# Moving both parts of split activations through TensorE as one 512-column operand in a two-block transformer kernel

## The chip, the cores and the metric

The kernel runs on one core of one Trainium2 chip. The metric is the device time in microseconds from one launch; lower is better. Every number below is from one profiled execution of the kernel before, or from the three timed runs beside it.

## The reference, cut to what matters

Two transformer blocks run on 256 tokens of width 1024, in float32. All the matrix products that the change touches are projections of the 256 tokens through a weight matrix:

```python
def first_block(x, ...):
    xn = rms_norm(x, norm1_w[l])
    z = xn @ w_in[l]                       # q, k, v, xr, gr, g_a, g_b
    attn = nsa_attention(q, ...)
    rnn = rg_lru_branch(xr, gr, ...)
    merged = jax.nn.sigmoid(g_a) * (attn @ w_up_attn[l]) + jax.nn.sigmoid(g_b) * (rnn @ w_up_rnn[l])
    x = x + merged @ w_out[l]
    hn = rms_norm(x, norm2_w[l])
    x = x + jnp.square(jax.nn.relu(hn @ mlp_w1[l])) @ mlp_w2[l]
    return rms_norm(x, final_norm_w)

def second_block(x, c, ...):
    for layer in range(2):
        sh1, sc1, g1, sh2, sc2, g2 = ...   # from c
        h = rmsnorm(x, norm_mix[layer]) * (1.0 + sc1) + sh1
        y = even_mixer(h, ...) if layer % 2 == 0 else odd_mixer(h, ...)   # both end in "@ w_out"
        x = x + g1 * y
        h = rmsnorm(x, norm_ffn[layer]) * (1.0 + sc2) + sh2
        x = x + g2 * peer_ffn(h, peer_w_q[layer], ...)                    # q = ht @ w_q, then 16384 experts
    return rmsnorm(x, norm_final)
```

## The kernel before, in words

**Layout.** Activations stand transposed: 128 features in the partitions, 8 chunks of features, 256 tokens in the columns. `T` is 256 and `KC` is 8.

**Split precision.** Every float32 operand is a sum of two fp32r tiles, an upper part and the rest. `Split` (L164 and after) loads a weight block of 128 x 8 x 128 with one DMA and makes two halves of it. For each half ScalarE casts the upper part (`wh`, L183) and VectorE subtracts it (`wl`, L184). The list `HI` (L39) says for each phase which share of the casts goes to VectorE instead (L181); only phase 5, the MLP, has a share, 0.4. The pools `ws` (5, and one more in most stages) hold the halves, so the two engines can be some halves ahead of TensorE.

**A product.** `mm3` (L195 to L199) takes three matmuls for one chunk: `wh` with the upper activations `hh` (L197), `wh` with the rest `hl` (L198), `wl` with `hh` (L199). Each has 256 columns, loads its own weights, and adds into the same 256 columns of a PSUM bank. I call three such matmuls a trio. `proj` runs the 8 trios of one block of 128 outputs into a bank of the pool `pm`, which has two banks; `proj_pairs` does the same for the mixers' output projections with 4 trios to a bank, because the 8 chunks come in two halves. After a block `filler()` advances side work by a rate: routing, gates, the ada products on GpSimd (L472), the recurrence.

**Who empties a bank.** In the gates (L788, L793) a VectorE copy; in `w_out` (L811) and `mlp2` (L875) one VectorE addition onto `x`; in the mixers' outputs (L1050, L1210) one VectorE multiply-add onto `x`; in the MLP's first product a ScalarE Relu (L865), then a VectorE square (L867) and a split into `hdh`, `hdl` (L240, L241); in the PEER query product a ScalarE copy (`evac`, L86).

**After `x`.** `norm_lead` makes from each chunk of `x` an upper part `rh` (ScalarE, L328) and a rest `rl` (VectorE, L329), takes squares (ScalarE, L253) and sums them (VectorE, L257). With `rh` and `rl` it runs four projections before the norm's factor is known (the leads), then makes `hh` and `hl`.

**Order.** Each engine runs its own list in a fixed order that is made when the kernel is built, from the order in the code and from what depends on what; so a later step is often placed among earlier ones of other chains.

**Memory.** `act_pair` gives two tiles, `hh` and `hl`. In the PEER part the same two places hold `av` (activations of experts read back from memory) in turn, and then `nat`.

Of the kernel before, what the change touches and what calls it, by code (L numbers as in the profile page):

```python
# [20 lines left out]
T = 256  # L21
# [17 lines left out]
HI = 0.0, 0.0, 0.0, 0.0, 0.0, 0.4, 0.0, 0.0  # L39
# [26 lines left out]
def build(tc, a, dbg=None):  # L66
    nc = tc.nc
    es = ExitStack()
    with es:
# [142 lines left out]

        def proj_nat(src, ah, al, n, o=None, pool_=None, head=None):

            o = o or [bank(pool_ or pm) for _ in range(2)]
            nb = src.shape[0]
            for g in range(nb):
                w = head if g == 0 and head is not None else Split(src[g], [128, 2, n])
                for k in range(2):
                    for tt in range(2):  # L220
                        ts = slice(tt * 128, tt * 128 + 128)
                        kk = 2 * g + k
                        mm3(o[tt][:, :n], ah[:, kk, ts], al[:, kk, ts], *w[k], kk == 0, kk == 2 * nb - 1)
                filler()
            return o

        def proj_pairs(src, ah, al, k0):

            for f in range(2 * src.shape[0]):
                if f % 2 == 0:  # L230
                    w = Split(src[f // 2], [128, 2, 4, 128])
                o = bank(pm)
                for k in range(4):
                    mm3(o[:, :T], *(x[:, k] for x in w[f % 2]), ah[:, k0 + k], al[:, k0 + k], k == 0, k == 3)
                if f % 2 == 1:
                    filler()
                yield f, o
# [146 lines left out]
        def act_pair():  # L384
            oh = act.tile([128, KC, T], F32R, tag="hh", name="hh")
            ol = act.tile([128, KC, T], F32R, tag="hl", name="hl")
            return oh, ol
# [129 lines left out]
        xh, xl = act_pair()  # L517

        with tc.tile_pool(name="fb", bufs=1) as fb, ExitStack() as fs:
# [266 lines left out]
            for c in range(KC):  # L786
                o = proj(win(16 + c), xh, xl)
                nc.vector.tensor_copy(gr[:, c], o[:, :T])  # L788
            ga = fb.tile([128, KC, T], F32, name="ga")
            gb = fb.tile([128, KC, T], F32, tag="gb", name="gb")  # L790
            for c in range(2 * KC):
                o = proj(win(24 + c), xh, xl)
                nc.vector.tensor_copy((ga if c < KC else gb)[:, c % KC], o[:, :T])  # L793
# [3 lines left out]
            mh, ml = act_pair()  # L797
# [11 lines left out]
            for f in range(KC):  # L809
                o = proj(a["w_out"][f], mh, ml)  # L810
                nc.vector.tensor_tensor(out=cur["x"][:, f], in0=o[:, :T], in1=cur["x"][:, f], op=ALU.add)  # L811
# [42 lines left out]
        hh, hl = act_pair()  # L854
        with tc.tile_pool(name="mlp", bufs=1) as mp:
# [4 lines left out]
            hdh = mp.tile([128, 32, T], F32R, name="hdh")  # L860
            hdl = mp.tile([128, 32, T], F32R, name="hdl")
            for c in range(32):
                o = m4[:, c] if c < 4 else proj(a["mlp1"][c] if c > 4 else w4, hh, hl)
                r = t1.tile([128, T], F32, tag="t", name="r")
                nc.scalar.activation(r, o[:, :T], AF.Relu)  # L865
                q = t1.tile([128, T], F32, tag="t", name="q")
                nc.vector.tensor_tensor(out=q, in0=r, in1=r, op=ALU.mult)  # L867
                split_act(hdh[:, c], hdl[:, c], q)
            with tc.tile_pool(name="toe", bufs=1) as toe:
                side = beside(toeplitz(toe), 0.5)  # L870
                for f in range(KC):
                    o = bank(pm)
                    for kg in range(4):
                        proj(a["mlp2"][4 * f + kg], hdh, hdl, k0=8 * kg, o=o, first=kg == 0, last=kg == 3)
                    nc.vector.tensor_tensor(out=cur["x"][:, f], in0=o[:, :T], in1=cur["x"][:, f], op=ALU.add)  # L875
# [20 lines left out]
        def even_mixer(lp, m, sh, gcol):  # L896
            with tc.tile_pool(name="ev", bufs=1) as ev, ExitStack() as es2:
# [4 lines left out]
                hh, hl = act_pair()  # L902
# [144 lines left out]
                def mixed(products, n):  # L1047

                    for f, o in islice(products, n):
                        nc.vector.scalar_tensor_tensor(out=cur["x"][:, f], in0=o[:, :T], scalar=gcol[:, f:f + 1],  # L1050
                                                       in1=cur["x"][:, f], op0=ALU.mult, op1=ALU.add)
# [12 lines left out]
                for h in range(4):  # L1064
                    if h < 3:
                        qk_diff(h + 1)
                    if h == 2:

                        mh, ml = act_pair()
                        for tt in range(2):  # L1070
                            to_mix(ew, aos[tt].rearrange("p h d -> p (h d)"), mh, ml, 0, tt)
                        halves = [proj_pairs(a["ew_out"][half], mh, ml, 4 * half) for half in range(2)]
# [51 lines left out]
        def odd_mixer(lp, m, sh, gcol):  # L1124
            with tc.tile_pool(name="od", bufs=1) as od, ExitStack() as es2:
# [3 lines left out]
                hh, hl = act_pair()  # L1129
# [30 lines left out]
                mh, ml = od.tile([128, KC, T], F32R, name="mh"), od.tile([128, KC, T], F32R, name="ml")  # L1160
# [47 lines left out]
                for half in range(2):  # L1208
                    for f, o in proj_pairs(a["ow_out"][half], mh, ml, 4 * half):
                        nc.vector.scalar_tensor_tensor(out=cur["x"][:, f], in0=o[:, :T], scalar=gcol[:, f:f + 1],  # L1210
                                                       in1=cur["x"][:, f], op0=ALU.mult, op1=ALU.add)
# [148 lines left out]
        def peer(lps, lp, l, m, sh, gcol):  # L1360
# [9 lines left out]
            hh, hl = act_pair()  # L1370
# [26 lines left out]
            for c in range(4, 16):  # L1397
                o = proj(a["peer_w_q"][l, c] if c > 4 else w4, hh, hl)
                evac(qT[:, c], o[:, :T])
# [40 lines left out]
            for n, i2 in enumerate((124, 125, 126, 127)):  # L1440
                weigh([(i2, abs_[i2 // 2][:, i2 % 2])], n == 0, False)
            for n, b in enumerate([15] + list(range(15))):
                m = 4 if b == 15 else 8
                av = act.tile([128, 8, T], F32, tag=("hh", "hl")[n % 2], name="av")
# [9 lines left out]
            nat = act.tile([128, 2, 2, 512], F32, tag="hh", name="nat")  # L1454
# [160 lines left out]
```

## Time and profile before

| | us |
|---|---|
| median of 3 timed runs | 2439.26 (2437.25 to 2440.48) |
| the profiled execution | 2435.75 |
| its span, first to last instruction | 2434.0 |
| TensorE busy in the span | 2361.3 (97%) |
| VectorE busy in the span | 2130.1 (88%) |
| ScalarE busy in the span | 1706.7 (70%) |
| GpSimd busy in the span | 726.0 (30%) |

The profile shows one execution. Between its span and its own time lie 1.75 us, and the median of the timed runs is 3.5 us above it. TensorE's busy time counts modelled ends, so two matmuls that follow each other overlap in it; how fast they follow is read from their starts. The same is true of VectorE and ScalarE in small measure: the next instruction can start before the one ahead is reported as ended.

### The profile page before, as it was taken

The page shows a single profiled execution, that of the slowest core. Times are in us where ns is not written, and L with a number is a line of the kernel's source. Part 1 is how long each engine was busy: PE and PEld are TensorE (multiplying, and loading weights), DVE is VectorE, ACT ScalarE, POOL GpSimd, SP SyncE. Part 2 cuts the span into 40 slices and gives each one's busy share as a digit, 9 for nine tenths or more (in the row PEclk, how much of TensorE's full clock was granted, in tenths as well). Part 3 has the DMA queues.
Part 4 walks back from the last instruction along what each step waited for, and adds up shares of the span by engine and source line. Part 5 has one row for each costly group of instructions (what it writes and reads, how often), then busy time and mean ns, then how long its engine had stood idle before and what let it go on. Part 6 is the DMA issues. An engine that isn't in the chain of part 4 may idle for free.

```text
span 2434.0 us, 47856 instructions
## 1 busy us (share of the span) xinstructions
PE 2361.3 (97%) x16270; PEld 2169.1 (89%) x16270; DVE 2130.1 (88%) x4805; ACT 1706.7 (70%) x3906; POOL 726.0 (30%) x669
## 2 busy tenths in 40 slices
PE   8999999999999999999999988999999999999998
PEld 8889999988999999998888877999999999888886
DVE  8888997978889999999999986698989999777776
ACT  7886654677655799986666676665569998555554
POOL 1232322332004466642222234200346665000000
PEclk9999999999999999999999999999999999999999
DMA  7536677665566565578888755456655566777773
GB/s 246 186 122 218 196 231 241 205 209 166 180 208 204 178 198 192 195 233 296 294 295 293 276 191 190 155 166 209 199 179 192 194 195 201 269 235 240 247 246 113
DMA packets 165045, 516.03 MB, mean 212 GB/s; under 512 B 19104, under 2 KB 24000, under 8 KB 160960
## 3 DMA queue, kind: packets, MB, share of 16 engines
q1 hardware_dynamic: 146944, 480.45, 60.0%
q10 hardware_dynamic: 17856, 32.51, 3.5%
q8 instruction: 129, 2.11, 0.4%
q14 instruction: 116, 0.95, 0.1%
HBM read 478.00 MB, written 34.34 MB: 210 GB/s over the span
## 4 chain that ended last, share of the span: by engine, by line
PE 75%; DVE 15%; ACT 4%; issue 3%; POOL 2%; DMA 1%; SPq 0%; ACTq 0%; DVEq 0%; POOLq 0%
PE bank L199 23%; PE bank L197 23%; PE bank L198 23%; DVE wl L184 5%; PE bank L1334 2%; DVE o L1346 1%; DVE G L1329 1%; ACT o L1348 1%; ACT wh L183 1%; PE bank L428 1%; PE bank L892 1%; POOL eq L1310 1%; POOL aw L472 1%; DVE hl L241 1%; PE bank L1183 1%
## 5 line engine op out<-in xcount | busy, mean ns | idle before, releaser
L183 ACT CAST wh<-w 128x512 fp32r<-128x512 f32 (+1 forms) x1443 | 871.1, 616 | 444.7 <-PE bank L198 243.5
L184 DVE TENSOR_TENSOR wl<-w,wh 128x512 fp32r<-128x512 f32 x1494 | 1056.5, 727 | 136.2 <-ACT wh L183 129.5
L197 PE MATMUL bank<-hh,wh 128*128 128x256 f32 x3112 | 889.9, 286 | 5.5 <-ACT ab L1407 2.8
L199 PE MATMUL bank<-hh,wl 128*128 128x256 f32 x3112 | 885.8, 285 | 7.0 <-DVE wl L184 6.7
L198 PE MATMUL bank<-hl,wh 128*128 128x256 f32 x3112 | 885.0, 284 | 6.4 <-DVE hl L241 5.6
L199 PEld LDWEIGHTS bank<-hh,wl 128*128 128x128 f32 x3112 | 596.4, 192 | 12.7 <-DVE wl L184 11.9
L197 PEld LDWEIGHTS bank<-hh,wh 128*128 128x128 f32 x3112 | 596.0, 192 | 13.1 <-ACT ab L1407 3.7
L198 PEld LDWEIGHTS bank<-hl,wh 128*128 128x128 f32 x3112 | 596.5, 192 | 10.0 <-DVE hl L241 7.9
L472 POOL TENSOR_TENSOR aw<-aw,sc 128x512 f32<-128x512 f32 x192 | 289.0, 1507 | 724.4 <-DMA aw<-in_ada 715.1
L199 PE MATMUL bank<-wh,w_l 128*128 128x512 f32 x1024 | 398.4, 389 | 0.0
L198 PE MATMUL bank<-wl,w_h 128*128 128x512 f32 x1024 | 398.4, 389 | 0.0
L197 PE MATMUL bank<-wh,w_h 128*128 128x512 f32 x1024 | 398.4, 389 | 0.0
L1344 POOL TENSOR_SCALAR o<-iota,i1T 128x128 fp32r<-128x128 f32 x384 | 327.5, 865 | 188.6 <-PE bank L1334 146.9
L197 PEld LDWEIGHTS bank<-wh,w_h 128*128 128x128 f32 x1024 | 192.2, 188 | 40.1
L199 PEld LDWEIGHTS bank<-wh,w_l 128*128 128x128 f32 x1024 | 192.2, 188 | 39.8 <-DVE w_l L241 0.2
L198 PEld LDWEIGHTS bank<-wl,w_h 128*128 128x128 f32 x1024 | 192.2, 188 | 39.8
L1348 ACT ACTIVATE o<-o,gq 128x128 fp32r<-128x128 f32 x512 | 183.0, 395 | 22.5 <-DVE o L1346 17.1
L1329 DVE TENSOR_TENSOR G<-bank,G 128x256 f32<-128x256 f32 x256 | 193.6, 757 | 0.0
L240 ACT CAST w_h<-W 128x256 fp32r<-128x256 f32 x256 | 103.2, 403 | 97.6 <-PE bank L198 94.5
L1346 DVE TENSOR_SCALAR o<-iota,i2T,gtT 128x128 fp32r<-128x128 f32 x512 | 161.8, 350 | 0.0
L1336 ACT COPY G<-bank 128x256 f32<-128x256 f32 x256 | 158.8, 647 | 1.2 <-PE bank L1334 0.9
L241 DVE TENSOR_TENSOR w_l<-W,w_h 128x256 fp32r<-128x256 f32 x256 | 126.1, 492 | 38.1 <-ACT w_h L240 37.9
(454 smaller groups left out, 3085.2 us busy)
## 6 DMA issues: line engine op xcount, KB each, us to landing
w<-in_peer_u SPq DMA_DIRECT2D x256, 512.0 KB, 4.1
w<-in_peer_v SPq DMA_DIRECT2D x256, 512.0 KB, 4.3
aw<-in_ada SPq DMA_DIRECT2D x192, 256.0 KB, 4.0
w<-in_mlp SPq DMA_DIRECT2D x64, 512.0 KB, 4.3
asp<-ab ACTq DMA_DIRECT2D x124, 256.0 KB, 3.4
av<-asp SPq DMA_DIRECT2D x30, 1024.0 KB, 7.1
w<-in_win_t SPq DMA_DIRECT2D x40, 512.0 KB, 4.2
w<-in_peer_w_q SPq DMA_DIRECT2D x32, 512.0 KB, 4.3
```

The costliest lines, as they stand in the source:

```text
L183: fill["cast"] = nc.scalar.copy(wh, wg).ins
L184: nc.vector.tensor_tensor(out=wl, in0=wg, in1=wh.bitcast(F32), op=ALU.subtract)
L197: nc.tensor.matmul(o, lhsT=sh, rhs=mh, start=first, stop=False, **kw)
L198: nc.tensor.matmul(o, lhsT=sh, rhs=ml, start=False, stop=False, **kw)
L199: fill["mm"] = nc.tensor.matmul(o, lhsT=sl, rhs=mh, start=False, stop=last, **kw).ins
L241: nc.vector.tensor_tensor(out=ol, in0=in_, in1=oh.bitcast(F32), op=ALU.subtract)
L472: nc.gpsimd.tensor_tensor(out=w, in0=w, in1=sil[:, 512 * q:512 * q + 512], op=ALU.mult)
L1329: nc.vector.tensor_tensor(out=Gp, in0=lo, in1=Gp, op=ALU.add)
L1336: nc.scalar.copy(Gp, S[:, :, :128])
L1344: (nc.vector if (t + r) % 8 in O1_DVE else nc.gpsimd).tensor_scalar(o1[:, r], iota, i1T[:, c], None, op0=ALU.is_equal)
L1346: nc.vector.tensor_scalar(o2[r][:, 0], iota, i2T[:, c], gh[:, c], op0=ALU.is_equal, op1=ALU.mult)
L1348: nc.scalar.activation(o2[r][:, 1], o2[r][:, 0].bitcast(F32), AF.Copy, scale=gq[:, c])
```

## The change

In six kinds of product (the gates `gr`, `ga`, `gb`; `w_out`; the MLP's two; the mixers' output projections; the PEER query) the two parts of the activations lie side by side in one tile, and one matmul of 512 columns moves both through `wh`. A second one of 256 columns moves the upper part through `wl` into the left half of the bank. The bank then holds two halves whose sum is the product. `add_halves` adds them: ScalarE copies the right half out, VectorE adds the left half to it. `to_x` adds or multiply-adds each half onto `x`, with two VectorE instructions. The MLP's Relu and square become one VectorE instruction. The cast share of phase 5 goes from 0.4 to 0. The tile of `act_pair` holds both parts under one tag, and `av` is two halves of one tile.

```diff
-HI = 0.0, 0.0, 0.0, 0.0, 0.0, 0.4, 0.0, 0.0
+HI = 0.0, 0.0, 0.0, 0.0, 0.0, 0.0, 0.0, 0.0
...
+        def proj_both(src, ab, k0=0, o=None, first=True, last=True, n=KC):
+            w = src if isinstance(src, Split) else Split(src, [128, n, 128])
+            if o is None:
+                o = bank(pm)
+            for k in range(n):
+                mm_both(o, *w[k], ab[:, k0 + k], first and k == 0, last and k == n - 1)
+            filler()
+            return o
+
+        def mm_both(o, wh, wl, ab, first, last):
+            nc.tensor.matmul(o, lhsT=wh, rhs=ab, start=first, stop=False, skip_group_check=True)
+            fill["mm"] = nc.tensor.matmul(o[:, :T], lhsT=wl, rhs=ab[:, 0], start=False, stop=last,
+                                          skip_group_check=True).ins
+
+        def add_halves(out, o):
+            nc.scalar.copy(out, o[:, T:])
+            nc.vector.tensor_tensor(out=out, in0=o[:, :T], in1=out, op=ALU.add)
+
+        def to_x(f, o, gcol=None):
+            x = cur["x"][:, f]
+            for q in range(2):
+                part = o[:, q * T:q * T + T]
+                if gcol is None:
+                    nc.vector.tensor_tensor(out=x, in0=part, in1=x, op=ALU.add)
+                else:
+                    nc.vector.scalar_tensor_tensor(out=x, in0=part, scalar=gcol[:, f:f + 1], in1=x, op0=ALU.mult,
+                                                   op1=ALU.add)
...
         def act_pair():
-            oh = act.tile([128, KC, T], F32R, tag="hh", name="hh")
-            ol = act.tile([128, KC, T], F32R, tag="hl", name="hl")
-            return oh, ol
+            both = act.tile([128, KC, 2, T], F32R, tag="h", name="h")
+            return both, both[:, :, 0], both[:, :, 1]
...
             for c in range(KC):
-                o = proj(win(16 + c), xh, xl)
-                nc.vector.tensor_copy(gr[:, c], o[:, :T])
+                add_halves(gr[:, c], proj_both(win(16 + c), xb))
...
             for f in range(KC):
-                o = proj(a["w_out"][f], mh, ml)
-                nc.vector.tensor_tensor(out=cur["x"][:, f], in0=o[:, :T], in1=cur["x"][:, f], op=ALU.add)
+                to_x(f, proj_both(a["w_out"][f], mb))
...
             for c in range(32):
-                o = m4[:, c] if c < 4 else proj(a["mlp1"][c] if c > 4 else w4, hh, hl)
-                r = t1.tile([128, T], F32, tag="t", name="r")
-                nc.scalar.activation(r, o[:, :T], AF.Relu)
                 q = t1.tile([128, T], F32, tag="t", name="q")
-                nc.vector.tensor_tensor(out=q, in0=r, in1=r, op=ALU.mult)
-                split_act(hdh[:, c], hdl[:, c], q)
+                if c < 4:
+                    r = m4[:, c]
+                else:
+                    r = t1.tile([128, T], F32, tag="t", name="r")
+                    add_halves(r, proj_both(a["mlp1"][c] if c > 4 else w4, hb))
+                nc.vector.scalar_tensor_tensor(out=q, in0=r, scalar=0.0, in1=r, op0=ALU.max, op1=ALU.mult)
+                split_act(hd[:, c, 0], hd[:, c, 1], q)
...
                     for kg in range(4):
-                        proj(a["mlp2"][4 * f + kg], hdh, hdl, k0=8 * kg, o=o, first=kg == 0, last=kg == 3)
-                    nc.vector.tensor_tensor(out=cur["x"][:, f], in0=o[:, :T], in1=cur["x"][:, f], op=ALU.add)
+                        proj_both(a["mlp2"][4 * f + kg], hd, k0=8 * kg, o=o, first=kg == 0, last=kg == 3)
+                    to_x(f, o)
...
                     for f, o in islice(products, n):
-                        nc.vector.scalar_tensor_tensor(out=cur["x"][:, f], in0=o[:, :T], scalar=gcol[:, f:f + 1],
-                                                       in1=cur["x"][:, f], op0=ALU.mult, op1=ALU.add)
+                        to_x(f, o, gcol)
...
             for c in range(4, 16):
-                o = proj(a["peer_w_q"][l, c] if c > 4 else w4, hh, hl)
-                evac(qT[:, c], o[:, :T])
+                add_halves(qT[:, c], proj_both(a["peer_w_q"][l, c] if c > 4 else w4, hb))
...
+            avs = act.tile([128, 2, 8, T], F32, tag="h", name="av")
             for n, b in enumerate([15] + list(range(15))):
                 m = 4 if b == 15 else 8
-                av = act.tile([128, 8, T], F32, tag=("hh", "hl")[n % 2], name="av")
+                av = avs[:, n % 2]
                 nc.sync.dma_start(out=av[:, :m], in_=asp[b][:, :m])
...
-            nat = act.tile([128, 2, 2, 512], F32, tag="hh", name="nat")
+            nat = act.tile([128, 2, 2, 512], F32, tag="h", name="nat")
```

The gates `ga`, `gb` and the odd mixer's output change in the same way as `gr` and the even mixer's.

## Rows read from the trace of the kernel before

**Rows 1.** The page: busy time of each engine.

```profile
PE 2361.3 (97%) x16270; PEld 2169.1 (89%) x16270; DVE 2130.1 (88%) x4805; ACT 1706.7 (70%) x3906; POOL 726.0 (30%) x669
```

**Rows 2.** Busy time by stretch: length, PE, PEld, DVE, ACT, POOL, clock, DMA.

```profile
136.00:207.00 71.00, 66.34 (x532) 61.21 (x531) 61.02 (x97) 57.58 (x121) 22.27 (x15) 0.98 0.43 145
286.00:362.00 76.00, 74.96 (x622) 74.50 (x622) 74.18 (x130) 43.27 (x112) 23.25 (x14) 1.00 0.71 233
362.00:455.00 93.00, 92.91 (x777) 92.15 (x776) 76.18 (x125) 43.77 (x101) 24.37 (x18) 1.00 0.75 232
600.00:624.00 24.00, 23.61 (x191) 22.76 (x189) 23.20 (x55) 19.74 (x47) 2.79 (x3) 1.00 0.47 135
624.00:660.00 36.00, 36.00 (x304) 35.98 (x303) 30.61 (x123) 20.15 (x39) 0.00 (x0) 1.00 0.58 190
```

**Rows 3.** PE's timeline, PEER query: start, duration; 1st and 51st matmul.

```profile
639.72 0.28 PE L197 MATMUL bank<-hh,wh 128*128 128x256 f32 x1
...
645.70 0.28 PE L199 MATMUL bank<-hh,wl 128*128 128x256 f32 x1
```

**Rows 4.** The same where experts are weighed: 1st and 27th matmul.

```profile
1099.65 0.39 PE L198 MATMUL bank<-wl,w_h 128*128 128x512 f32 x1
...
1105.54 0.39 PE L197 MATMUL bank<-wh,w_h 128*128 128x512 f32 x1
```

**Rows 5.** By source line: ns minimum/median/maximum, first and last start.

```profile
L811 DVE TENSOR_TENSOR xT<-bank,xT x8: 411/418/425, 244.2 to 265.5; 128x256 f32<-128x256 f32 x8
L1210 DVE SCALAR_TENSOR_TENSOR xT<-bank,mod,xT x16: 471/478/485, 1564.8 to 1590.0; 128x256 f32<-128x256 f32 x16
L86 ACT COPY qT<-bank x24: 366/367/378, 624.3 to 1642.0; 128x256 f32<-128x256 f32 x24
L867 DVE TENSOR_TENSOR q<-r x32: 410/417/1544, 275.7 to 366.7; 128x256 f32<-128x256 f32 x32
```

**Rows 6.** DVE's timeline at the end of the odd mixer's output: start, duration.

```profile
1590.00 0.48 DVE L1210 SCALAR_TENSOR_TENSOR xT<-bank,mod,xT 128x256 f32<-128x256 f32 x1
1590.40 0.48 DVE L329 SCALAR_TENSOR_TENSOR rl<-xT,m,rh 128x256 fp32r<-128x256 f32 x1
1590.79 0.42 DVE L257 TENSOR_TENSOR acc<-acc,sq 128x256 f32<-128x256 f32 x1
1591.12 0.69 DVE L184 TENSOR_TENSOR wl<-w,wh 128x512 fp32r<-128x512 f32 x1
1591.73 0.49 DVE L329 SCALAR_TENSOR_TENSOR rl<-xT,m,rh 128x256 fp32r<-128x256 f32 x1
```

**Rows 7.** What DVE waited for in 1564 to 1592: us, times, longest.

```profile
DVE xT L1210 <- PE bank L199: 0.9, 2, 0.5
DVE ao L1204 <- PE bank L892: 0.8, 1, 0.8
```

**Rows 8.** PE's timeline in the first lead after it: start, duration.

```profile
1591.47 0.28 PE L198 MATMUL bank<-rl,wh 128*128 128x258 f32 x1
1591.87 0.39 PE L199 MATMUL bank<-rh,wl 128*128 128x258 f32 x1
...
1592.94 0.28 PE L198 MATMUL bank<-rl,wh 128*128 128x258 f32 x1
```

**Rows 9.** DVE's timeline where the even mixer's output ends.

```profile
604.17 0.48 DVE L1050 SCALAR_TENSOR_TENSOR xT<-bank,mod,xT 128x256 f32<-128x256 f32 x1
605.89 0.48 DVE L329 SCALAR_TENSOR_TENSOR rl<-xT,m,rh 128x256 fp32r<-128x256 f32 x1
```

**Rows 10.** Groups by line: casts on DVE, busy us, mean ns.

```profile
L181 DVE CAST wh<-w 128x512 fp32r<-128x512 f32 x51 | 26.6, 524 | 0.4
```

**Rows 11.** The page's DMA issues: KB each, us to landing.

```profile
av<-asp SPq DMA_DIRECT2D x30, 1024.0 KB, 7.1
```

**Rows 12.** By tile, as in rows 5: the MLP's hidden tile, read and written.

```profile
L197 PEld LDWEIGHTS bank<-hdh,wh x256: 186/188/192, 362.4 to 454.5; 128*128 128x128 f32 x128
...
L240 ACT CAST hdh<-q x32: 389/407/409, 278.1 to 367.2; 128x256 fp32r<-128x256 f32 x32
```

## What I expect of the change, and from which rows

> **What bounds the kernel now.** I read the page first: TensorE is busy for 97% of the span and VectorE for 88% [rows 1]. That says that TensorE is the first suspect, and no more, since its ends are modelled. So I read next the busy time by stretch, cut where the changed products lie [rows 2]. In the second MLP product and in the PEER query TensorE has no idle time. But VectorE is busy 74.18 of 76 us in the first MLP product and 23.20 of 24 us after the even mixer's output. The reader is to see two engines near their limits there: what TensorE gains is kept only where VectorE and ScalarE, which feed it with split weights and empty its banks, have time to spare. The granted clock is 1.00, the upper level of 2.4 GHz, in all these stretches but the gates (0.98). Third, the starts in TensorE's timeline give the pace of matmuls, which busy time can't: 50 steps in 5.98 us, 0.1196 us for 256 columns [rows 3], and 26 steps in 5.89 us, 0.2265 us for 512 columns [rows 4]. Twice 0.1196 less 0.2265 is 0.0127 us: every matmul costs that much beside its columns, and each of these loads its own weights.
>
> **The gain on TensorE.** A trio takes 3 x 0.1196 = 0.3588 us now and 0.2265 + 0.1196 = 0.3461 us after, 0.0127 us less. The trios, from the loops: gates 24 x 8 = 192, `w_out` 64, first MLP product 28 x 8 = 224, second 256, even mixer's output 64, odd mixer's 64, PEER query 2 x 96 = 192. That makes 1056, and 13.4 us. By stage: 2.4, 0.8, 2.8, 3.3, 0.8, 0.8 and 1.2 twice. No row shows 512 and 256 columns in turn; the nearest rows are these two, and I see no reason for more or less than their sum.
>
> Here a rule speaks against the change. The Trainium skill, "TensorE: Matmul & The Clock Gate", section "Back-to-back issue gap", gives a warm step as the columns over 2.4 GHz plus 2.5 ns. By it a trio would lose 2.5 ns and the sum would be 1056 x 0.0025 = 2.6 us. The rows say 12.7 ns, so the trace does not agree, and the rows are taken.
>
> **What it adds, stage by stage.** The price of a copy on ScalarE out of a bank is 0.367 us, of an addition from a bank on VectorE 0.418 us, of a multiply-add 0.478 us [rows 5]. VectorE starts its next instruction before the last has ended: a multiply-add holds it for 1590.40 - 1590.00 = 0.40 us and a 256-column addition for 0.33 us [rows 6]. A step that needs the result of the one ahead can take its full 0.48 us; both are in the ranges.
>
> *Gates.* VectorE's copy becomes an addition, which costs it nothing. ScalarE gets 24 copies, 8.8 us, of which 16, 5.9 us, fall where it has 71 - 57.58 = 13.4 us idle [rows 2]. They fit, but they stand in one list with the casts and with attention's exponentials, so a bank comes free later. I keep 1.0 of the 2.4 us. Bounds: all 2.4 kept, or half of the copies on the path, 4.4 - 2.4 = 2 us lost.
>
> *`w_out`.* Eight more additions, 2.6 to 3.3 us on VectorE, against some two to five casts of 0.524 us [rows 10] that leave it as the phase changes, and 0.8 us on TensorE. I put the stage at 0, from -1.5 to +1.5.
>
> *First MLP product.* 622 matmuls are 25.9 blocks, so VectorE works 74.18 / 25.9 = 2.86 us for each [rows 2]. It loses 0.8 casts, 0.42 us [rows 10], and gains an addition, 0.42 us; the fused square costs what L867 does, 0.417 us in the median [rows 5], to 0.478 us. So it stays at 2.86 us, while TensorE would want 8 x 0.3461 = 2.77 us. TensorE can run down the halves that are split ahead, and then takes VectorE's pace. I keep half, 1.4 us; bounds 2.8 gained and 0.5 lost.
>
> A rule bears on the addition's price here. VectorE's operations on two SBUF operands are stretched by GpSimd's: L867 takes 410 to 1544 ns, while the steps that read a bank stay within 411 to 485 ns [rows 5]. The Trainium skill, "SBUF — State Buffer", section "Who interferes with whom", says that a VectorE instruction with at most one SBUF input does not contend with GpSimd. The trace agrees; if it did not hold, each added step could cost up to 1.5 us, and the mixers would lose some 17 us each.
>
> *Second MLP product.* VectorE has 93 - 76.18 = 16.8 us idle and loses 26 casts, 13.4 us; ScalarE takes them with 49 us idle [rows 2, 10]. Cover is ample; the last `x` comes 0.4 us later. I keep 2.9 of 3.3 us; bounds 3.3 and 2.0.
>
> *Odd mixer's output.* Here VectorE decides. A block is only four trios, 1.44 us. In that time VectorE splits one half of weights, 0.60 us by the step from 1591.12 to 1591.73, steps `x`, 0.40 us, and towards the end makes `rl`, 0.39 us, and a sum, 0.33 us [rows 6]: 1.72 us, more than TensorE's 1.44, paid out of halves split ahead. The change adds 16 x 0.40 = 6.4 us, and VectorE waited for 0.9 + 0.8 = 1.7 us there [rows 7], so it comes out 4.7 us late, or 2.7 us if the six sums of squares are put off. The end has no cushion: the lead's matmul at 1591.87 starts 0.40 us after the one ahead, not 0.12, because the split of 1591.12 ends just then, and the last `rl`, done at 1592.22, is used at 1592.94, 0.7 us later [rows 6, 8]. Net 2.0 to 4.0 us lost after the lead; I take 2.7. TensorE's 0.8 us only makes it wait sooner. Lower bound: 0.8 gained.
>
> *Even mixer's output.* The same 6.4 us, more of it among attention where VectorE waits. Its end is as tight: the last `x` step is at 604.17 and a last `rl` at 605.89 [rows 9], in a stretch that is 97% busy [rows 2]. I take 2.4 lost, from 0.8 gained to 4.0 lost.
>
> *PEER query, twice.* Twelve additions hold VectorE 12 x 0.33 = 4.0 us, and it has 36 - 30.61 = 5.4 us idle in a stretch that gets 1.2 us shorter [rows 2]. It just fits. I keep 0.9 of 1.2 us each; bounds 1.2 gained, 0.8 lost.
>
> `av` in one tile costs nothing if a part of a tile can be read while another is written. It can: `hdh` is read from 362.4, and still written at 367.2 [rows 12].
>
> **The sum.** -1.0 + 0 - 1.4 - 2.9 + 2.7 + 2.4 - 1.8 = -2.0 us on a profiled execution of 2435.75 us, 2433.7 after. The median of the runs shown is 2439.26, 3.5 us above; carried over, 2437.
>
> **The rivals.** *TensorE's gain is kept nearly whole.* The order is made anew, and sums and later splits may make room for the added steps; VectorE's idle time in the gates and the second MLP product speaks for it, the full stretches against. With the mixers at no loss and little lost elsewhere it is 9 to 13 us, 2426 to 2430. Chance 0.30.
>
> *VectorE becomes the bound: slower.* If the two steps onto `x` wait for each other, a block of a mixer's output needs 0.60 + 0.48 + 0.48 = 1.56 us of VectorE against TensorE's 4 x 0.3461 = 1.38. It decides once no half is split ahead any more. Then each mixer loses its upper bound, 4.0 us, with `w_out` 1.5, the gates 2.0 and the query 1.6, against 2.9 and 0 from the MLP: +10 us at most, about +5 to +10, 2444 to 2449. Chance 0.17.
>
> *It doesn't save what it says.* If the fixed part is not paid per matmul but per column group, the trio saves 2.6 us in all, or nothing. The mixers' 5.1 us stay, the other stages give about 1: 2443. The page named above gives this time; the rows' two widths speak against it. Chance 0.05.
>
> *`av` loses its second buffer.* If one tile lets no load start before the other half is read, 30 loads show up to 7.1 us each [rows 11], 200 us. Rows 12 speak against it. Chance 0.02.
>
> **How the numbers follow.** 0.2%, 4.9 us, is about what a measurement of this kernel can tell from no change: 2434.4 to 2444.1. The forecast has 0.46, over 2432 to 2442; some 0.07 of it lies below 2434.4. Faster: 0.30 + 0.07 = 0.37. Slower: 0.17 + 0.02, and little of the third: 0.19. Same: 0.44. The range 2427 to 2446 leaves out the best part of the first rival, the worst of the second, and the last.
>
> **What would show it.** Right: steps of 0.2265 and 0.1196 us in turn in TensorE's timeline; the second MLP product about 3 us shorter; VectorE without idle time in both mixers' outputs, and TensorE waiting for `rl` or `wl` in the first lead after each. Wrong: no such waits (then the first rival), waits for banks in the MLP or the gates (the second), trios of 0.356 us (the third), or ones for `av` (the last).

## The result: 0.8% slower, and the profile after

The changed kernel takes 2459.89 us in the median against 2439.07 us, a ratio of 1.0082 (95% interval 1.0068 to 1.0097), some 20 us. The forecast was 2437. The profiled execution has a span of 2455.3 us, against 2434.0 before. The page's busy times answer to [rows 1]:

```profile
PE 2367.3 (96%) x15214; PEld 2119.8 (86%) x15214; DVE 2146.0 (87%) x4854; ACT 1738.1 (71%) x3975; POOL 721.7 (29%) x669
```

TensorE has 1056 matmuls fewer and is busy 6 us longer. Work that got smaller can't do that by itself. The busy time of the stretch where the even mixer's output ends says why (columns as in [rows 2]; counted back from the norm's spread behind the lead, its counterpart of before is 576 to 611):

```profile
594.00:602.00 8.00, 5.00 (x29) 4.03 (x28) 7.46 (x17) 5.89 (x13) 3.85 (x3) 0.94 0.46 149
602.00:607.00 5.00, 4.78 (x21) 3.91 (x20) 3.53 (x7) 1.77 (x5) 1.73 (x1) 0.75 0.57 203
607.00:617.00 10.00, 8.94 (x47) 6.79 (x45) 9.08 (x26) 9.48 (x26) 0.00 (x0) 1.00 0.15 53
617.00:622.00 5.00, 3.45 (x16) 3.28 (x17) 5.00 (x12) 2.60 (x6) 0.00 (x0) 0.62 0.15 46
622.00:630.00 8.00, 8.00 (x45) 8.00 (x45) 3.44 (x8) 2.19 (x5) 0.00 (x0) 0.60 0.68 221
```

The reader is to see two pairs. TensorE has idle time in the first stretch (5.00 of 8 us busy), and the granted clock is 0.75 in the next. It has idle time again from 617, and the clock stays near 0.6 until 630, that is, mostly at the lower level of 1.2 GHz. Before, it was 1.00 there, and TensorE was busy for 33.23 of 35 us:

```profile
576.00:611.00 35.00, 33.23 (x262) 31.02 (x261) 32.07 (x77) 28.51 (x73) 8.17 (x6) 1.00 0.48 146
```

What TensorE waited for from 594 to 630 in the changed kernel (us, times, longest):

```profile
PE bank L225 <- DVE h L1153: 2.4, 1, 2.4
PE bank L199 <- DVE wl L184: 1.5, 1, 1.5
PE bank L197 <- DVE xT L242: 1.0, 1, 1.0
```

All three are VectorE's results. The last two fall into the first lead after the output. Its start in TensorE's timeline (start, duration; in brackets the idle time ahead):

```profile
615.54 0.36 PE L197 MATMUL bank<-rh,wh 128*128 128x258 f32 x1
...
617.05 0.36 PE L197 MATMUL bank<-rh,wh 128*128 128x258 f32 x1 [1.04 <-DVE xT L242]
619.02 0.58 PE L199 MATMUL bank<-rh,wl 128*128 128x258 f32 x1 [1.49 <-DVE wl L184]
619.40 0.42 PE L197 MATMUL bank<-rh,wh 128*128 128x258 f32 x1
...
620.05 0.42 PE L197 MATMUL bank<-rh,wh 128*128 128x258 f32 x1
```

The trio from 619.40 to 620.05 takes 0.65 us; at the upper level one takes 0.36 [rows 3]. And VectorE's timeline beside it, the counterpart of [rows 6]:

```profile
616.43 0.48 DVE L242 SCALAR_TENSOR_TENSOR xT<-bank,mod,xT 128x256 f32<-128x256 f32 x1
616.82 0.48 DVE L366 SCALAR_TENSOR_TENSOR rl<-xT,m,rh 128x256 fp32r<-128x256 f32 x1
617.22 0.42 DVE L294 TENSOR_TENSOR acc<-acc,sq 128x256 f32<-128x256 f32 x1
617.55 0.48 DVE L366 SCALAR_TENSOR_TENSOR rl<-xT,m,rh 128x256 fp32r<-128x256 f32 x1
617.95 0.42 DVE L294 TENSOR_TENSOR acc<-acc,sq 128x256 f32<-128x256 f32 x1
618.28 0.69 DVE L184 TENSOR_TENSOR wl<-w,wh 128x512 fp32r<-128x512 f32 x1
```

The second step onto `x` is one 0.40 us place in this list, and the weights' split at 618.28, for which TensorE stands from 617.5 to 619.02, is behind all of them.

Read by the starts of the norms' spreads in the two traces, the even mixer's stretch grew from 120.8 to 135.1 us and the odd one's from 151.1 to 154.0. But kernels that are alike in a stretch differ there by up to 6 us from one profiled execution to the next. In the part from the first spread to the one ahead of the first MLP product it is 252.2 us before and 254.9 in a kernel changed only behind it; in six kernels with the old mixers' outputs (the one before, `no_mixers` and four others below) the even mixer takes 119.5 to 125.6 us and the odd one 147.2 to 151.3. The odd mixer's 151.1 before is near the top of that, so 2.9 us is probably too little for its growth. So the pieces were measured as kernels of their own.

### The profile page after: what moved, and what is told of

Same layout as the page of the kernel before. It is cut to its first block, busy times and chain, and to the rows that moved or that the text cites. A ratio compares the mean times of both kernels' runs of the same rounds, so it can differ in the third digit from the quotient of the medians.

```text
span 2455.3 us, 45783 instructions
## 1 busy us (share of the span) xinstructions
PE 2367.3 (96%) x15214; PEld 2119.8 (86%) x15214; DVE 2146.0 (87%) x4854; ACT 1738.1 (71%) x3975; POOL 721.7 (29%) x669
## 4 chain that ended last, share of the span: by engine, by line
PE 60%; DVE 10%; ACT 3%; issue 2%; POOL 2%; DMA 1%; ACTq 0%; DVEq 0%; SPq 0%; POOLq 0%
PE bank L199 17%; PE bank L197 17%; PE bank L198 17%; DVE wl L184 4%; PE bank L225 2%; PE bank L1369 2%; DVE o L1381 2%; DVE G L1364 2%; PE bank L226 1%; ACT o L1383 1%; PE bank L928 1%; POOL eq L1345 1%; POOL aw L509 1%; PE bank L1219 1%; PE bank L1275 1%
## 5 line engine op out<-in xcount | busy, mean ns | idle before, releaser
L183 ACT CAST wh<-w 128x512 fp32r<-128x512 f32 x1494 | 903.7, 617 | 450.7 <-PE bank L198 180.7
L184 DVE TENSOR_TENSOR wl<-w,wh 128x512 fp32r<-128x512 f32 x1494 | 1067.3, 734 | 137.9 <-ACT wh L183 132.9
L197 PE MATMUL bank<-h,wh 128*128 128x256 f32 x2376 | 679.2, 286 | 5.3 <-ACT ab L1441 2.9
L199 PE MATMUL bank<-h,wl 128*128 128x256 f32 x2376 | 676.7, 285 | 6.4 <-DVE wl L184 6.2
L198 PE MATMUL bank<-h,wh 128*128 128x256 f32 x2376 | 675.1, 284 | 2.1 <-DVE h L278 1.5
L199 PEld LDWEIGHTS bank<-h,wl 128*128 128x128 f32 x2376 | 455.8, 192 | 11.7 <-DVE wl L184 10.6
L197 PEld LDWEIGHTS bank<-h,wh 128*128 128x128 f32 x2376 | 455.3, 192 | 10.9 <-ACT ab L1441 3.7
L198 PEld LDWEIGHTS bank<-h,wh 128*128 128x128 f32 x2376 | 455.8, 192 | 3.8 <-DVE h L278 2.7
L225 PE MATMUL bank<-h,wh 128*128 128x512 f32 x736 | 268.8, 405 | 11.3 <-DVE h L278 4.9
L226 PE MATMUL bank<-h,wl 128*128 128x256 f32 x736 | 209.1, 285 | 2.1 <-DVE wl L184 2.0
L225 PEld LDWEIGHTS bank<-h,wh 128*128 128x128 f32 x736 | 139.6, 190 | 49.8 <-DVE h L278 7.5
```

The source lines that it names most:

```text
L183: fill["cast"] = nc.scalar.copy(wh, wg).ins
L184: nc.vector.tensor_tensor(out=wl, in0=wg, in1=wh.bitcast(F32), op=ALU.subtract)
L197: nc.tensor.matmul(o, lhsT=sh, rhs=mh, start=first, stop=False, **kw)
L198: nc.tensor.matmul(o, lhsT=sh, rhs=ml, start=False, stop=False, **kw)
L199: fill["mm"] = nc.tensor.matmul(o, lhsT=sl, rhs=mh, start=False, stop=last, **kw).ins
L225: nc.tensor.matmul(o, lhsT=wh, rhs=ab, start=first, stop=False, skip_group_check=True)
```

## The experiments

Theory A: VectorE's added steps at the mixers' outputs hold back the splits, TensorE stands idle, and its clock falls. B: the 512-column matmul waits for both parts of the activations, and the order is made anew. C: the new matmuls are slow by themselves.

**Where the loss lies.** `no_mixers` has the new form everywhere but in the mixers' outputs; `mixers_only` has it there alone.

```
 no_mixers:    halves = [proj_pairs(a["ew_out"][half], mh, ml, 4 * half) ...]      (no mb; odd mixer too)
               nc.vector.scalar_tensor_tensor(out=x[:, f], in0=o[:, :T], ...)      (in place of to_x)
 mixers_only:  the kernel before, with proj_pairs(..., mb) and to_x(f, o, gcol) in both mixers
```

> The changed kernel with the two mixers' outputs as they were before (three matmuls of 256 columns, one multiply-add on VectorE per block); the gates, the attention's output, both MLP products and the PEER query stay changed. The traces put 14.2 us of the loss between the even mixer's first and last lead (490.1 to 611.0 before, 494.4 to 629.5 after) and 2.9 us in the odd mixer (1445.5 to 1596.7, 1464.5 to 1618.6). If the mixers' outputs carry them, this kernel comes to about 2459.9 - 17.1 = 2443, a ratio to before of about 1.0015. If the loss in the even mixer's stage is carried in from the stages before it (a shifted order of the work), it stays at 2455 or above.

> The kernel before with the new form in the two mixers' outputs alone (512-column operand, two multiply-adds per block). If the loss is made there: 2439.1 + 17.1 = 2456, ratio about 1.007. If it is carried in from the earlier stages: within 4 us of before.

Measured: 2445.82 us, ratio 1.0012 (0.9997 to 1.0026), and 2455.94 us, 1.0063 (1.0043 to 1.0082). The mixers' outputs carry about 15 us of the 20 and aren't burdened by what precedes them. The other five edits together, forecast at -7.1 us, come out at -0.7 to +6.3. Such figures are the ratio's interval applied to 2439 us; differences of the medians can come out some 4 us otherwise, here +6.8 against the ratio's +2.9.

Where in the mixers? In the trace of `mixers_only` the first lead after the even mixer, from its first matmul to the norm's spread, is 11.0 us long, against 7.2 before:

```profile
612.55 0.36 PE L197 MATMUL bank<-rh,wh 128*128 128x258 f32 x1
...
623.59 0.60 PE L321 MATMUL bank<-dg,ones 128*128 128x128 f32 x4
```

```profile
603.76 0.28 PE L197 MATMUL bank<-rh,wh 128*128 128x258 f32 x1
...
610.99 0.49 PE L284 MATMUL bank<-dg,ones 128*128 128x128 f32 x3
```

The one after the odd mixer is 10.3 us against 7.0. Together the leads lose 7.1 us, of which about 4 are TensorE's waits for `x` and `wl`; the clock is lower behind them in both. The rest of the 15 us, about 8, lies ahead of the leads.

**What in the mixers' outputs.** `mixers_one_step` leaves out the second multiply-add; `before_two_steps` adds one to the old form.

```
 mixers_one_step:   for q in range(2 if gcol is None else 1):      (to_x)
 before_two_steps:  scalar_tensor_tensor(out=x[:, f], in0=o[:, :T], scalar=gcol[:, f:f + 1], in1=x[:, f], ...)
+                   scalar_tensor_tensor(out=x[:, f], in0=o[:, :T], scalar=0.0, in1=x[:, f], op0=mult, op1=add)
```

> The changed kernel with only the first of the two multiply-adds per block of the mixers' outputs: the second half of each bank, the product of the activations' lower part, is left out of the result. The matmuls and the operand of 512 columns stay. Theory A (VectorE's 32 added steps, 0.40 us each, hold back the splits of the weights, TensorE starves, and its clock falls): most of the mixers' 17.1 us come back, 2443 to 2446. Theory B (the first 512-column matmul of a block waits for both parts of the activations, and the order of the work is another): nothing much comes back, 2455 to 2460. Theory C (the 512-column matmuls are slower than the three small ones in this stage): nothing comes back either.

> The kernel before, with a second VectorE step of the same size behind each multiply-add of the two mixers' outputs: it reads the same half of the bank, multiplies it by zero and adds x, so the result stays. The matmuls stay the three small ones. Theory A: the price of the steps shows without any change of the matmuls, and more than in the changed kernel is not expected: 2447 to 2456. Theories B and C: 2439 to 2442, since only 16 + 16 steps of 0.40 us are added on an engine that they take to have room.

Measured: 2445.22 us, 1.0025 (1.0009 to 1.0041), and 2455.05 us, 1.0057 (1.0041 to 1.0073). Theory A. Without any new matmul, 32 VectorE steps cost 13.9 us (10.0 to 17.8), as much as the whole edit within the intervals; without the steps, the new matmuls cost what `no_mixers` costs, within the intervals. B and C are not needed for the 15 us. The busy time of `before_two_steps` has both falls of the clock, with the old matmuls:

```profile
598.00:602.00 4.00, 2.10 (x11) 1.67 (x11) 3.46 (x6) 2.29 (x6) 1.56 (x2) 0.87 0.52 172
602.00:606.00 4.00, 4.00 (x26) 3.99 (x26) 2.03 (x5) 1.21 (x3) 1.17 (x1) 0.71 0.47 158
...
612.00:618.00 6.00, 3.92 (x28) 3.35 (x28) 5.88 (x16) 5.68 (x13) 0.00 (x0) 1.00 0.01 3
618.00:622.00 4.00, 3.74 (x19) 3.74 (x20) 4.00 (x9) 0.74 (x2) 0.00 (x0) 0.57 0.41 137
```

`mixers_one_step` keeps an early one (0.59 from 594 to 598, after a wait of 2.3 us for `h` L1153, the lower part of the mixed activations: that is B, and its cost can't be told from zero, since this kernel and `no_mixers` agree within the intervals) and loses the late one:

```profile
594.00:598.00 4.00, 4.00 (x15) 3.43 (x16) 2.20 (x3) 1.28 (x3) 1.22 (x1) 0.59 0.89 306
...
612.00:618.00 6.00, 6.00 (x52) 6.00 (x52) 5.22 (x14) 2.77 (x7) 0.75 (x1) 1.00 0.84 257
```

**The other edits one by one**, each the kernel before with the new form in one place (`mlp2_query` in two).

```
 mlp2_query:  proj_both(a["mlp2"][...], hd, ...), to_x(f, o); add_halves(qT[:, c], proj_both(a["peer_w_q"]...))
 mlp1_only:   add_halves(r, proj_both(a["mlp1"][c] ..., hb)), the fused square, HI[5] = 0.0
 gates_only:  add_halves(gr[:, c], proj_both(win(16 + c), xb)) and the same for ga, gb
 w_out_only:  to_x(f, proj_both(a["w_out"][f], mb))
```

> The kernel before with the new form in the second MLP product (256 trios of matmuls) and in the PEER query (2 x 96 trios) alone. By the prediction's steps: -2.9 - 0.9 - 0.9 = -4.7 us, a ratio of 0.998. By the pace of the trios in the two traces (second MLP 0.3589 before, 0.3558 after; query 0.362 before, 0.354 after): 256 x 0.003 + 192 x 0.008 = 2.3 us off, a ratio of 0.999.

> The kernel before with the new form in the first MLP product alone (and the casts of the weights all on ScalarE, as in the change). By the prediction's step: -1.0 us, ratio 0.9996. If VectorE is what this stage waits for (84.1 of 86 us busy before, 85.8 of 88 after), the added step per block stands against the casts that leave it, and TensorE's gain goes into waiting: 2439 to 2443, ratio 1.000 to 1.0015.

(The prediction's step for the first MLP product was -1.4 us; the figure quoted here is wrong.)

> The kernel before with the new form in the 24 blocks of the gates alone. By the prediction's step: -1.0 us (range -2.4 to +2), ratio 0.9996. If VectorE holds this stage as it holds the mixers' outputs: up to +3 us (the stretch before the second lead is 252.2 us before, 255.4 after), ratio 1.001.

> The kernel before with the new form in the attention's output alone: 8 blocks, 8 added steps of VectorE, with a norm's lead behind them as at the mixers' ends. By the prediction's step: 0 (-1.5 to +1.5). If each end with two steps per block pays as the mixers' do (16 added steps for 14.2 and 2.9 us): +1.5 to +7 us, and TensorE's granted clock falls behind it; in the changed kernel's trace it does not fall there (1.00 from 270 to 300), so +1.5 to +3 is the likelier part, ratio 1.001.

| kernel | median us | ratio (95% interval) | us against 2439 | forecast |
|---|---|---|---|---|
| second MLP product and query | 2435.42 | 0.9990 (0.9979 to 1.0001) | -2.4 (-5.1 to +0.2) | -4.7 |
| first MLP product | 2439.39 | 1.0005 (0.9994 to 1.0015) | +1.2 (-1.5 to +3.7) | -1.4 |
| gates | 2441.14 | 1.0011 (0.9999 to 1.0022) | +2.7 (-0.2 to +5.4) | -1.0 |
| `w_out` | 2444.27 | 1.0023 (1.0010 to 1.0036) | +5.6 (+2.4 to +8.8) | 0 |
| both mixers' outputs | 2455.94 | 1.0063 (1.0043 to 1.0082) | +15.4 (+10.5 to +20.0) | +5.1 |

The us are the ratio's, as above. They sum to +22.5 us, against +20 for all at once. `w_out` pays for 8 steps what the mixers pay for some 12, in the middle of its interval.

For the gates the trace shows a thing that is not in the sum of costs at all: the order of VectorE's and GpSimd's instructions around attention is another. VectorE's timeline in `gates_only`:

```profile
143.73 1.07 DVE L184 TENSOR_TENSOR wl<-w,wh 128x512 fp32r<-128x512 f32 x1
...
146.43 1.78 DVE L184 TENSOR_TENSOR wl<-w,wh 128x512 fp32r<-128x512 f32 x1
148.13 4.97 DVE L725 TENSOR_TENSOR_SCAN xc<-av,ig 128x256 f32<-128x256 f32 x3
153.03 1.26 DVE L795 TENSOR_REDUCE mn<-bank 128x2 f32<-128x512 f32 x2
```

GpSimd's, beside it:

```profile
144.22 1.74 POOL L509 TENSOR_TENSOR aw<-aw,sc 128x512 f32<-128x512 f32 x1
145.92 5.04 POOL L722 TENSOR_TENSOR ig<-ig,rg 128x512 f32<-128x512 f32 x3
```

The recurrence's products come three in a row, the three scans stand behind them and ahead of attention's minimum at 153.03, and TensorE waits for the exponentials. Before, its longest wait here is another and shorter:

```profile
PE bank L465 <- ACT P L799: 5.2, 1, 5.2
```

```profile
PE bank L733 <- DVE ce L731: 3.7, 1, 3.7
```

All five kernels with the new gates have the wait of 5.2 us, all eleven with the old ones that of 3.7. The clock behind it does not divide them so. From 144 to 170 it is 0.74 in `gates_only`, the changed kernel and `no_mixers`, 0.80 in `filled_wait`, but 0.93 in `mixers_one_step`, which has the new gates and the long wait; with the old gates it is 0.80 to 0.93. In order `gates_only`, `mixers_one_step`, `before_two_steps`:

```profile
144.00:170.00 26.00, 20.81 (x104) 15.65 (x105) 20.84 (x26) 16.75 (x39) 9.84 (x7) 0.74 0.23 78
144.00:170.00 26.00, 20.45 (x129) 16.54 (x128) 21.12 (x30) 19.07 (x45) 9.48 (x7) 0.93 0.27 86
144.00:170.00 26.00, 21.21 (x126) 17.66 (x127) 20.56 (x30) 17.62 (x39) 11.26 (x8) 0.80 0.37 122
```

That the 2.7 us come from the longer wait is possible, not shown: the interval touches zero.

**Is the fall of the clock a cause or a sign?** `filled_wait` is the changed kernel with matmuls put into the two idle places at 615.8 and 617.4.

```
 (first lead of the PEER query, k = 0 and 1, behind the two matmuls with wh)
+for j in range((10, 13)[k]):
+    nc.tensor.matmul(o[:m, 258:512], lhsT=wh, rhs=rh[:, k, :254], start=True, stop=True)
 (the two matmuls with wl behind both)
```

> The changed kernel, with 23 matmuls of 254 columns added in the first lead of each of the two PEER queries (they write unused columns of a bank and change nothing in the result): 10 behind the first pair of matmuls and 13 behind the second, where TensorE stands idle for 1.04 and 1.49 us in the changed kernel's trace (at 615.8 to 617.05 and 617.4 to 619.02). If the clock that TensorE is granted falls because it stands idle there, the lead behind runs at the higher level: the trios from 619 on take 0.36 instead of 0.64 us, about 2.8 us come back behind the even mixer and 1.5 behind the odd one, 2455 to 2457. If the fall has another cause, or the lead is paced by VectorE at that point anyway: 2459 to 2463.

Contrary to that text, the added matmuls do change the kernel's result, so it is read for its times alone. TensorE's timeline:

```profile
616.57 1.34 PE L381 MATMUL bank<-rh,wh 128*128 128x254 f32 x10
...
617.98 1.68 PE L381 MATMUL bank<-rh,wh 128*128 128x254 f32 x13
620.08 0.28 PE L377 MATMUL bank<-rh,wh 128*128 128x258 f32 x1
...
620.43 0.28 PE L377 MATMUL bank<-rh,wh 128*128 128x258 f32 x1
```

With the idle time filled the clock is 1.00 from 616 to 626, and the trio at 620.08 takes 0.35 us, not 0.65. From the lead's first matmul to the norm's spread it is 616.26 to 626.0, 9.8 us, against 615.54 to 629.5, 14.0 us, although 2.7 us of matmuls were added. So in this lead the fall follows from the idle time, and filling it gives back 4.2 us. How much such a fall costs varies: `mixers_only` has the same two waits, 1.03 and 1.49 us, and its lead is 11.0 us long, not 14.0. In the lead after the odd mixer the filling gives next to nothing, 9.9 us against 10.2. For the whole kernel it stays open: the median, 2456.75 us, is 3.1 below the changed kernel's and lies in the range expected for this cause, but the ratio, 1.0084 (1.0069 to 1.0099), is not below 1.0082, and the intervals are wider than what is asked. That holding the clock pays is therefore shown for one lead, not for the kernel.

**Where in the outputs, and how it grows.** The added step of `before_two_steps` in the first 8 blocks of each mixer, in the last 8, and twice in all 16.

```
 steps_first:         if half == 0: scalar_tensor_tensor(... scalar=0.0 ...)
 steps_last:          if half == 1: scalar_tensor_tensor(... scalar=0.0 ...)
 before_three_steps:  the added step twice
```

> The kernel before with the second VectorE step (product by zero, result unchanged) in the first 8 of each mixer's 16 output blocks only. If the loss is made where no weights lie split ahead, at the end of the outputs, these 16 steps cost little: 2439 to 2443. If VectorE is full through the whole of both outputs, each step costs its own 0.40 us wherever it stands: about 2439 + 8 = 2447, half of what the 32 steps cost.

> The same in the last 8 blocks only. If the loss is made at the end: nearly all of the 16 us of the 32 steps, 2451 to 2455. If VectorE is full throughout: about 2447.

> The kernel before with two added steps per block of the mixers' outputs, 64 in all. If VectorE had some room and the first 32 steps used it up, the second 32 cost more than the first 32 did (16 us): above 2471. If it was full from the first step: about the same again, 2468 to 2472. If the first 32 cost a fixed price (one fall of the clock per end): less, 2457 to 2466.

Measured: 2448.90 us, 1.0042 (1.0026 to 1.0059); 2443.59 us, 1.0027 (1.0016 to 1.0038); 2459.50 us, 1.0095 (1.0078 to 1.0112). In us: +10.2 (6.3 to 14.4), +6.6 (3.9 to 9.3), both together +14, twice +23 (19.0 to 27.3). (The first expectation has 8 us for 16 steps of 0.40; that makes 6.4, so 2445.) Both intervals hold 6.4: the steps are paid wherever they stand, the early ones no less than the late ones. The theory of a loss at the end alone is wrong. On the growth the expectation missed: 2459.50 us lies in the range given for a fixed price, and below both others. The first 32 steps cost 0.43 us each and the next 32 cost 0.29; the intervals, some 4 us each way, don't tell these two apart. A price that is wholly fixed doesn't fit either, since the second 32 still cost about 9 us; that a part of the first 14 us is fixed stays possible.

Nor is the clock needed for a loss: in `steps_first` it is 1.00 through both outputs and both leads, in stretches of 3 us, and the leads take 7.2 and 7.1 us, as before. The longest waits of TensorE in that kernel's even mixer, for attention's `P`, are no longer than before, where they sum to 3.2 us from 490 to 611. What grew are the waits for the steps onto `x`, 1.4 us in the even mixer and 2.6 in the odd one, against 0.3 before (and 1.4 us for `hh` in the even mixer). First `steps_first`, even and odd mixer, then before, even mixer:

```profile
PE bank L428 <- DVE P L1099: 3.1, 4, 1.0
PE bank L197 <- DVE xT L1053: 1.4, 2, 0.9
...
PE bank L197 <- DVE xT L1216: 2.6, 3, 1.0
```

```profile
PE bank L428 <- DVE P L1096: 3.2, 4, 1.5
PE bank L197 <- DVE xT L1050: 0.3, 1, 0.3
```

These make some 5 of the 10 us; where the others lie isn't shown.

**The other direction.** Is VectorE alone the bound there? `before_fewer_steps` leaves out the multiply-adds of the first 8 blocks. `split_on_pool` is `mlp2_query` with every fourth lower part of the mixers' weights made on GpSimd.

```
 before_fewer_steps:  if half == 1: scalar_tensor_tensor(out=x[:, f], ...)
 split_on_pool:       (nc.gpsimd if n % 4 == 0 else nc.vector).tensor_tensor(out=wl, in0=wg, in1=wh, op=subtract)
```

> The kernel before without the multiply-adds of the first 8 of each mixer's 16 output blocks: 16 VectorE steps fewer, and that half of the mixers' outputs is missing from the result. 16 steps added at the same place cost 10 us (ratio 1.0042). If VectorE alone sets the pace of this stretch, the 16 steps taken away give about as much back: 2430 to 2434, ratio 0.996 to 0.998. If VectorE and TensorE are both full there in the kernel before (both 100% busy in the last 10 us before the lead's end), adding costs and taking away gives little: 2436 to 2439, ratio 0.999 to 1.000.

> A version that might beat both: the kernel before with the new form in the second MLP product and the PEER query alone (ratio 0.999), and with every fourth lower part of the weights of the mixers' outputs taken on GpSimd, which stands idle at those ends, in place of VectorE: 16 splits of 0.68 us leave VectorE. If VectorE alone sets the pace there: 2428 to 2432, ratio 0.996. If both engines are full, or VectorE's steps beside a GpSimd step take longer (1.07 to 1.78 us for a step of 0.68 us beside GpSimd's in the gates' trace): 2436 to 2442, ratio 0.999 to 1.001.

Measured: 2442.67 us, 1.0002 (0.9987 to 1.0017), and 2437.18 us, 0.9993 (0.9978 to 1.0007). Sixteen steps added cost 10 us; sixteen taken away at the same place give nothing that can be measured, with an interval of -3.2 to +4.1 us against their own 6.4. So before the change VectorE alone doesn't set the pace of the stretch. That TensorE fills it too, and that a step added to VectorE is paid for this reason, fits both results. VectorE's wait for banks in `before_fewer_steps` shows where its freed time went (3.0 us from 580 to 632, against 0.2 before from 580 to 612):

```profile
L1051 DVE SCALAR_TENSOR_TENSOR xT<-bank,mod,xT 128x256 f32<-128x256 f32 x8 | 3.8, 480 | 3.0 <-PE bank L199 3.0
```

The version with the lowest median is `mlp2_query`, whose interval ends at 1.0001; a gain of 0.1% is likely and not certain. GpSimd's help adds nothing to it that can be measured.

## Why the prediction was wrong, by its own steps

**The gain on TensorE** was right where it was read and too large elsewhere. In the PEER query of the changed kernel 19 trios take 6.60 us, 0.3474 each, against the 0.3461 forecast:

```profile
653.09 0.39 PE L225 MATMUL bank<-h,wh 128*128 128x512 f32 x1
653.33 0.28 PE L226 MATMUL bank<-h,wl 128*128 128x256 f32 x1
...
659.69 0.39 PE L225 MATMUL bank<-h,wh 128*128 128x512 f32 x1
```

That is 0.0114 us saved of the 0.0127, and the third rival falls for this stretch. The rule of 2.5 ns that the prediction set against the change is no test of this stretch: the Trainium skill, "TensorE: Matmul & The Clock Gate", section "Back-to-back issue gap", gives that formula for an isolated matmul, and says that in a stream of weight loads and matmuls both set the spacing. In the second MLP product the saving is smaller. Ten trios, first the changed kernel, then the one before:

```profile
419.95 0.39 PE L225 MATMUL bank<-hd,wh 128*128 128x512 f32 x1
...
423.47 0.39 PE L225 MATMUL bank<-hd,wh 128*128 128x512 f32 x1
```

```profile
420.05 0.28 PE L197 MATMUL bank<-hdh,wh 128*128 128x256 f32 x1
...
423.63 0.28 PE L197 MATMUL bank<-hdh,wh 128*128 128x256 f32 x1
```

0.352 against 0.358 us: 0.006 saved in these ten. From the first to the last of its matmuls the product takes 92.1 to 93.0 us in the ten kernels with the old form and 90.9 to 91.8 in the six with the new: about 1 us, 0.004 a trio, which is nearer to the third rival's 0.0025 than to the forecast. The prediction took the pace of the 256-column matmul from the query for all stages. Two of the three matmul pairs of a trio are at 0.116 to 0.117 us in the median in this product, and the 512-column matmul takes 0.233, not 0.2265. So about 1 us was there to be had, not 3.3, and the sign of a product 3 us shorter did not come; with the query's 192 x 0.0114 = 2.2 us it makes some 3, and 2.4 were measured.

**The mixers' outputs** are the step that failed: +5.1 us forecast, +15.4 measured. Half of it was right, the end: the lead without cushion, with `wl` and the steps onto `x` that TensorE waits for, as the prediction's list of signs has them. In `mixers_only` the two leads lose 3.8 and 3.3 us, within the bounds of 4.0. What failed is the cover. The step set 1.7 us of VectorE's waits and the sums put off against 6.4 us of added work, and of the even mixer it said that more of the steps lie among attention, where VectorE waits; so the steps ahead of the end stood at nothing. `steps_first` shows that those early steps are paid in full, 10.2 us for 16, with both leads as before. Idle time of an engine whose instructions stand in a list was no cover here for a step that comes at another place in it. A second thing was missing from the bound: it was the shortage of VectorE alone, and nothing stood there for what a wait does to TensorE's clock. In the changed kernel's even lead, 14.0 us against 7.2 before, the two waits make 2.5 and the lower clock most of the rest.

**`w_out`** was put at 0 and costs +5.6 us (+2.4 to +8.8). The sum of VectorE's time against casts that leave it did not hold. Where the 5.6 us lie is not shown: the profiled execution of `w_out_only` took 2438.25 us, 6 below that kernel's median. It has new waits for the steps onto `x`, 0.6 and 0.3 us from 240 to 290, so the mixers' mistake a second time is likely.

**Gates and the first MLP product**, -1.0 and -1.4 forecast, came out at +2.7 and +1.2 with intervals that reach the forecasts' upper part or just contain them. For the gates the prediction looked for late banks; the trace shows a list in another order and a longer wait, without a loss that is clear of the noise. For the first MLP product the reading that VectorE's pace stays and TensorE's gain has nowhere to go fits better than the half that was kept.

**The rivals.** "VectorE becomes the bound" named the mechanism and the point from which it decides, and had its price wrong: 2444 to 2449, since its bounds for the mixers and for `w_out` were the ones above. "Kept nearly whole" is excluded. `av` in one tile did nothing: the two PEER layers take 835.0 and 828.6 us from spread to spread, 834.6 and 829.2 before.

## What to carry to other kernels

Where two engines are both near their limits in a stretch, price each added instruction at no less than the whole time for which it holds its engine, wherever in the stretch it stands, and don't count on getting as much back from one taken away. Trading matmuls for steps of the engine that feeds them can pay only where that engine has idle time next to the place of the step; in the second MLP product and the query, which have it, the trade cost nothing that could be measured and may have gained 2.4 us. Behind every forecast wait of TensorE, allow for trios at the lower clock, read from a stretch of the trace that has such a wait. And read an execution's waits beside several kernels that are alike there: the clock behind the gates and attention's `P` looked like causes until the other traces were laid beside them.

## What the runs showed of the hardware that was not expected

After a wait of 1.0 us and one of 1.5 close behind it, the granted clock was at the lower level of 1.2 GHz for about the next 9 us of the changed kernel, but only for about the next 3 of `before_two_steps` (0.65 us per trio in place of 0.36); 23 matmuls without use in the idle time kept it at 2.4 GHz. VectorE's split of 0.68 us took 1.07 to 1.78 us beside GpSimd's products in the gates' stretch; the Trainium skill, "SBUF — State Buffer", section "Who interferes with whom", has the two engines contend where VectorE reads two SBUF operands and GpSimd reads SBUF too, and the trace agrees. The same 256-column matmul, with a weight load each, steps at 0.116 to 0.120 us depending on the stretch; the cause wasn't looked for.
